# Hybrid decoder step: 128x128 transpositions taken from TensorE, done as 32x32 turns on VectorE and copies through DRAM

## The chip, the cores and the metric

The kernel runs on one core of a Trainium2 chip. The metric is the device time of one execution in microseconds. The median of three runs of the kernel before is 2550.52 us (2545.99 to 2553.72). Its profiled execution took 2546.89 us and has a span of 2545.2 us, from its first instruction to its last.

## The reference, cut to what matters

One layer of a decoder with 16 heads of three kinds over 1024 prompt tokens with 16 meta tokens before them, and 64 sample tokens (8 sequences of 8). All is fp32.

```
h = rmsnorm(x) * norm_w                       # tokens x 2048
proj = h @ w_in                               # 2048 x 8984: q, k, v, o, gates, z of all heads
A, 6 heads: mLSTM scan in chunks (q, k, v, i, f), times sigmoid(o)
B, 6 heads: causal conv of 4, silu, l2norm; gated delta rule (triangular solve per chunk)
C, 4 heads: HGRN2 scan (q, forget f, v)
hcat = concat(A, B, C); hcat *= rsqrt(mean(hcat**2 per head) + eps)
y = hcat * out_norm_w * silu(z)
out = rmsnorm(x + y @ w_out) * final_norm_w   # the states at the end are outputs too
```

## The kernel before, in words

The tokens go in two halves: half 0 has 512 prompt tokens, the 64 sample tokens and the 16 meta tokens (592 columns), half 1 the other 512. The projection keeps channels on partitions and tokens along the columns. A column tile of 128 weights takes four pieces of `w_in` (each 512 x 128, one DMA of 256 KB, `w_raw`, L229). A piece is split into a rounded part `whi` (ScalarE) and a rest `wlo` (VectorE) in `feed_split` (L252). `run_group` (L293) multiplies each 128 x 128 block three times (`whi` with both parts of the input, `wlo` with the first): 24 matmuls of 288 or 304 columns a piece in half 0, 12 of 512 columns in half 1. The splits run up to three pieces ahead of the matmuls and the loads up to seven (`feed_ahead`, L273), in four buffers each. After both halves' projections comes the output product with `w_out` (`oacc`, L1694 on).

Everything else is woven between these matmuls. Each head's scan, its finish and the preparation of half 1's input are Python generators; `Weave` (L145) has four queues of them and lets the first of each take a step, one `yield` long, whenever its due time has come on a planner's clock (`Clock`, L85). The clock adds estimated costs of the instructions written so far; a step is due `LATENCY` = 0.4 us after the last result of the step before, and a step can add to that (`ck.last += 2.0`). `start_head` (L1528) drains the scan of the head before the last and all finishes: there the steps follow each other with no projection matmuls between. All matmuls and transpositions stand in TensorE's one list, all loads and stores in SP's one list, and each engine works through its list in order. All line numbers in the profile's rows are those of a recording helper (L136) for compute, and of the kernel's own line for DMAs.

Where a scan wants tokens on partitions, the tile with channels on partitions is turned by `T.transpose` (a TensorE instruction with the identity, 128 x 128 each) into PSUM, and copied or combined from there. The places that the change touches, per head and half of 512 tokens four transpositions each, and in half 0 one more for the 80 sample and meta tokens:

- `finish` (L799): the normed head outputs `hr` are turned back to channels on partitions (`py`, L818), and VectorE makes `y` from `py`, the weight and the gate `zs` (L820).
- `mlstm_scan` (L924): the values (`pv`, L960; ScalarE copies them to `v1`, L963) and the output gate (`pot`, L971; ScalarE adds 1, L973).
- `hgrn_scan` (L1361): the values (`pvh`, L1462).
- `prep_B` (L598): 16 blocks of half 1's normed input (`pt`, L358), which are split in two parts and stored to DRAM (`hb_dram`), from where `load_hB` (L1596) fetches them before half 1.

Of the kernel before, what the change touches and what calls it, by code (L numbers as in the profile page):

```python
# [189 lines left out]
def hybrid_step(ctx, tc, i, o):  # L190
# [25 lines left out]
    def bank(name):  # L216
        return ps.tile([P, 512], F32, tag="ps", name=name)
# [377 lines left out]
    hb_dram = [dp.tile([NG, P, 4, WB], F32R, name=f"hb{part}") for part in ("hi", "lo")]  # L595


    def prep_B():  # L598
        def load(c, g):
            x = sp.tile([P, 512], F32, tag="px", name="px", bufs=3)  # L600
            DMA(x, i["x_prompt"][0, HALF + P * c:HALF + P * (c + 1), 512 * g:512 * (g + 1)])
            return x

        stats = []
        items = [(c, g) for c in range(NC) for g in range(NG)]
        nxt = load(*items[0])
        for n, (c, g) in enumerate(items):
# [12 lines left out]
        for n, (c, g) in enumerate(items):  # L620
            x = nxt
            if c == 0:
                nw = load_nw(sp.tile([P, 512], F32, tag="pxs", name="pnw", bufs=1), g)
            if n + 1 < len(items):
                nxt = load(*items[n + 1])
            ck.last = ck.t["T"] + 6.0
            yield
            norm_apply(x, P, nw, stats[c])
            ck.last += 2.5
            yield  # L630
            src = transposed(x, P)
            lo = sp.tile([P, 512], F32R, tag="px", name="hblo", bufs=3).rearrange("p (k t) -> p k t", t=P)
            hi = x.bitcast(F32R).rearrange("p (k t) -> p k t", t=P)
            S.copy(hi, src)
            V.tensor_tensor(lo, src, hi, op=ALU.subtract)
# [149 lines left out]
    def evac(half, acc, tag, name, scale=None, func=AF.Copy):  # L785
# [5 lines left out]
                S.activation(t[:, off:off + cnt], a, func, scale=scale)  # L791
        return t

    def square_sums(g, src, ssq):
        for c in range(g.nt):
            scr = sq("scr", "scrq", bufs=1)
            S.activation(scr[:g.n], src[:, c], AF.Square, accum_out=ssq[0:g.n, g.at + c:g.at + c + 1])

    def finish(half, head, outs, ssq, scale, zs):  # L799
        r = sp.tile([P, 16], F32, tag="hr", name="hr")  # L800
        for g in half.groups:
            V.tensor_scalar(r[0:g.n, g.idx], ssq[0:g.n, g.idx], scale / P, EPS, op0=ALU.mult, op1=ALU.add)
            G.tensor_tensor(r[0:g.n, 8 + g.at:8 + g.at + g.nt], r[0:g.n, g.idx], halfneg[0:g.n, 0:g.nt], op=ALU.pow)
        yield
        hrs = []
        for g, hx in zip(half.groups, outs):
# [3 lines left out]
            hrs.append(hr)  # L810
        ck.last += 2.0
        yield
        W = half.width
        y = row("j", "y")
        for g, hr in zip(half.groups, hrs):
            py = bank("py")
            for c in range(g.nt):
                T.transpose(py[:, g.n * c:g.n * (c + 1)], hr[0:g.n, c], ident[0:g.n, 0:g.n])  # L818
            cs = slice(g.c0, g.c0 + g.width)
            V.scalar_tensor_tensor(y[:, cs], py[:, 0:g.width], onw[:, head:head + 1], zs[:, cs], op0=ALU.mult, op1=ALU.mult)  # L820
        yield
        yhi, ylo = zs.bitcast(F32R), y.bitcast(F32R)
        S.copy(yhi[:, 0:W], y[:, 0:W])
        yield
        G.tensor_tensor(ylo[:, 0:W], y[:, 0:W], yhi[:, 0:W], op=ALU.subtract)
        yield
        d = y_dram[half.index][head].bitcast(F32)
        for part, t in enumerate((yhi, ylo)):
            t = t.bitcast(F32)
            at_ = 2 * NSAMP if half.first else 0  # L830
            DMA(d[:, at_ + HALF * part:at_ + HALF * (part + 1)], t[:, 0:HALF])
            if half.first:
                DMA(d[:, NSAMP * part:NSAMP * (part + 1)], t[:, HALF:WS])
# [90 lines left out]
    def mlstm_scan(half, h, kT, qT, vT, tho, zs, nm, em, st):  # L924
# [25 lines left out]
        for g in half.groups:  # L950
            n = g.n
            pk = bank("pk")
            for c in range(g.nt):
                T.transpose(g.psum(pk)[:, c], g.col(kT, c), ident)
            kw = kwall[:, g.idx]
            V.tensor_tensor(kw[0:n], g.psum(pk), gate_col(half, g, K_W, h), op=ALU.mult)
            kws.append(kw)
            pv = bank("pv")
            for c in range(g.nt):
                T.transpose(g.psum(pv)[:, c], g.col(vT, c), ident)  # L960
            v1 = gt("2", g, P + 1)
            G.memset(v1[0:n, :, P:P + 1], 1.0)
            S.copy(v1[0:n, :, 0:P], g.psum(pv))  # L963
            v1s.append(v1)
        ck.last += 2.5
        yield
        for g in half.groups:
            n = g.n
            po = bank("pot")
            for c in range(g.nt):  # L970
                T.transpose(g.psum(po)[:, c], g.col(tho, c), ident)  # L971
            og = gt("3", g)
# [388 lines left out]
    def hgrn_scan(half, h, kT, lf, qT, vT, zs, st):  # L1361
# [181 lines left out]
    def done_tile(half, name, what, acc):  # L1543
# [8 lines left out]
        if what == "z":  # L1552
            t["z"] = no_meta(half, silu_evac(half, acc, "e", "zs"))
            if half.first:
                src = {"A": "state_mlstm_C", "B": "state_gdn_S", "C": "state_hgrn_S"}[kind]
                c["st"] = src
        elif kind == "A":
            if what == "o":
                t["o"] = no_meta(half, evac(half, acc, "d", "tho", scale=0.5, func=AF.Tanh))
            else:  # L1560
                t[what] = evac(half, acc, {"k": "a", "q": "b", "v": "c"}[what], what + "T", scale=KSCALE if what == "k" else None)
                if what == "q":
                    no_meta(half, t[what])
        elif kind == "B":
            weave.drain_queue("post")
            weave.drain(conv_stream)
            ei = {"q": h, "k": HB + h, "v": 2 * HB + h}[what]
            U = conv_evac(half, acc, ei)
            t[what] = row({"k": "c", "q": "d", "v": "f"}[what], "C" + what)
            c["posts"].append(weave.add("post", conv_post(half, U, ei, t[what]), lag="V"))  # L1570
        else:
            if what == "f":
                cf = evac(half, acc, "f", "cf")[:, 0:half.width]
                t["k"], t["f"] = row("a", "hk"), row("g", "lf")
                c["posts"].append(weave.add("post", hgrn_keys(half, h, cf, t["k"], t["f"]), lag="SV"))
            elif what == "q":
                t["q"] = no_meta(half, silu_evac(half, acc, "b", "hq"))
            else:
                t["v"] = evac(half, acc, "c", "hvT")
# [194 lines left out]
```

## Time and profile before

| what | number |
|---|---|
| median of three runs | 2550.52 us (2545.99 to 2553.72) |
| profiled execution, its span | 2546.89 us, 2545.2 us |
| granted TensorE clock, mean | 0.996 of full speed |
| half 0 (0 to 1215 us), TensorE busy | 1171.53 us of 1215 |
| half 1's projections (1215 to 2125 us), TensorE busy | 903.10 us of 910 |
| output product (2125 to 2546 us), TensorE busy | 407.77 us of 421 |
| VectorE, ScalarE busy in half 1's projections | 485.54 us, 368.39 us |

The busy time of an engine is the time covered by at least one of its instructions. Matmuls overlap each other, so a group's busy time and its time per instruction are not what the engine would save without it; that is read from the starts of the instructions around it. "Idle before" is the engine's gap ahead of an instruction, put down to what ended it.

### The profile page before, as it was taken

Reading aid. Unit: us, or ns where it says so; the run is one execution under the profiler, and the core shown is the slowest. Engines: PE = TensorE matmul, PEld = TensorE weight load, DVE = VectorE, ACT = ScalarE, POOL = GpSimd, SP = SyncE. Lnnn points to the kernel's source line nnn. Section 1 sums busy time; section 2 is a strip of 40 time slices with the busy share of each in tenths; the row PEclk is TensorE's granted clock in tenths of the full one; section 3 lists DMA queues with packets and bytes.
Section 4 is the critical chain, followed back from the end, with each engine's and each line's share of the span. In section 5 each row is a group of like instructions: output and inputs, shape, how many; then the busy total and the mean of one; then the engine's idle time right before and its main releaser. Section 6 shows DMA issues by size and latency. Waiting matters only on the chain.

```text
span 2545.2 us, 43177 instructions
## 1 busy us (share of the span) xinstructions
PE 2482.4 (98%) x16022; PEld 2226.0 (87%) x16022; DVE 1376.3 (54%) x2881; ACT 1024.0 (40%) x2512; POOL 552.8 (22%) x722
## 2 busy tenths in 40 slices
PE   6899999999999999999999999999999999999998
PEld 5899999999999999999788888888888888888886
DVE  7665655665745655546754556454554545422435
ACT  5733434343434334334643434333443435322324
POOL 5331212320313312203320103110320102211201
PEclk9999999999999999999999999999999999999999
DMA  5634433555634343436443334433343438436735
GB/s 128 170 91 113 121 85 90 153 154 151 161 79 117 92 119 88 110 88 185 125 118 101 103 99 109 109 98 96 102 106 95 110 97 271 140 84 189 261 97 182
DMA packets 458319, 317.19 MB, mean 125 GB/s; under 512 B 56740, under 2 KB 402428, under 8 KB 457084
## 3 DMA queue, kind: packets, MB, share of 16 engines
q1 hardware_dynamic: 458108, 314.43, 45.7%
q8 instruction: 126, 2.06, 0.3%
q14 instruction: 85, 0.70, 0.1%
HBM read 268.93 MB, written 45.42 MB: 124 GB/s over the span
## 4 chain that ended last, share of the span: by engine, by line
PE 80%; issue 5%; DMA 4%; DVE 4%; POOL 3%; ACT 2%; SPq 0%; POOLq 0%; DVEq 0%; ACTq 0%
PE acc L136 59%; PE oacc L136 8%; PE pa L136 1%; DVE wlo L136 1%; PE po L136 1%; PE pyy L136 1%; PE pz L136 1%; POOL res L136 1%; PE pu L136 1%; PE nd L136 1%; POOL X L136 1%; DMA wraw<-in_w_in_dram 1%; PE poh L136 1%; DMA wraw<-in_w_out_dram 1%; DMA x<-in_x_prompt_dram 1%
## 5 line engine op out<-in xcount | busy, mean ns | idle before, releaser
L136 DVE TENSOR_TENSOR wlo<-wraw,whi 128x512 fp32r<-128x512 f32 x720 | 534.2, 746 | 639.4 <-ACT whi L136 628.3
L136 PE MATMUL acc<-hA,whi 128*128 128x288 f32 (+1 forms) x4544 | 822.9, 303 | 16.1 <-ACT whi L136 10.1
L136 ACT CAST whi<-wraw 128x512 fp32r<-128x512 f32 x720 | 442.2, 618 | 899.0 <-PE acc L136 584.1
L136 PE MATMUL acc<-hB,whi 128*128 128x512 f32 x2272 | 723.3, 400 | 1.5 <-ACT whi L136 1.5
L136 PEld LDWEIGHTS acc<-hA,whi 128*128 128x128 f32 x4544 | 675.4, 190 | 23.2 <-ACT whi L136 12.3
L136 PE MATMUL acc<-hA,wlo 128*128 128x288 f32 x2240 | 487.9, 298 | 0.2 <-DVE wlo L136 0.2
L136 PEld LDWEIGHTS acc<-hB,whi 128*128 128x128 f32 x2272 | 408.8, 188 | 79.7 <-ACT whi L136 3.4
L136 PE MATMUL acc<-hB,wlo 128*128 128x512 f32 x1120 | 439.7, 393 | 2.0 <-DVE wlo L136 2.0
L136 PEld LDWEIGHTS acc<-hA,wlo 128*128 128x128 f32 x2240 | 366.0, 189 | 1.5 <-DVE wlo L136 1.4
L136 PE MATMUL oacc<-whi,y 128*128 128x512 f32 x1088 | 343.8, 390 | 1.2 <-ACT whi L136 1.1
L136 PEld LDWEIGHTS acc<-hB,wlo 128*128 128x128 f32 x1120 | 210.2, 188 | 51.5 <-DVE wlo L136 5.6
L136 PEld LDWEIGHTS oacc<-whi,y 128*128 128x128 f32 x1088 | 204.3, 188 | 44.3 <-ACT whi L136 2.4
L136 PE MATMUL oacc<-wlo,y 128*128 128x512 f32 x576 | 224.6, 390 | 0.8 <-DVE wlo L136 0.7
L136 PEld LDWEIGHTS oacc<-wlo,y 128*128 128x128 f32 x576 | 108.2, 188 | 24.4 <-DVE wlo L136 2.3
L136 POOL TENSOR_TENSOR res<-res,fnw 128x512 f32<-128x512 f32 (+1 forms) x34 | 53.1, 1589 | 259.0 <-ACT oscr L136 259.0
L136 POOL TENSOR_TENSOR qd<-qT,emb 128x512 f32<-128x512 f32 x12 | 16.8, 1401 | 363.7 <-PE po L136 363.7
L136 POOL TENSOR_TENSOR y<-y,zs 128x592 fp32r<-128x592 f32 (+1 forms) x32 | 47.1, 1471 | 143.6 <-ACT zs L136 143.6
L136 DVE TENSOR_TENSOR Yt<-Yc,Bb 128x60 f32<-128x60 f32 (+8 forms) x180 | 36.9, 205 | 51.2 <-DMA Bb<-db 46.5
L136 POOL TENSOR_TENSOR hr<-hr,halfneg 128x4 f32<-128x4 f32 (+1 forms) x48 | 47.2, 984 | 56.0 <-DVE hr L136 55.0
L136 POOL TENSOR_TENSOR X<-Ex,hk 128x256 f32<-128x256 f32 (+1 forms) x40 | 38.5, 963 | 93.2 <-PE pa L136 75.5
L136 POOL TENSOR_TENSOR nrm<-nrm,halfneg 128x10 f32<-128x10 f32 x12 | 23.5, 1956 | 129.3 <-DVE nrm L136 129.3
L136 DVE TENSOR_TENSOR Sx<-Sx,lf 128x256 f32<-128x256 f32 (+2 forms) x60 | 34.0, 569 | 26.9 <-ACT Ex L136 24.9
(410 smaller groups left out, 2839.6 us busy)
## 6 DMA issues: line engine op xcount, KB each, us to landing
wraw<-in_w_in_dram SPq DMA_DIRECT2D x564, 256.0 KB
wraw<-in_w_out_dram SPq DMA_DIRECT2D x144, 256.0 KB
y<-y SPq DMA_DIRECT2D x16, 576.0 KB
px<-in_x_prompt_dram SPq DMA_DIRECT2D x32, 256.0 KB
out_dram<-sst SPq DMA_DIRECT2D x16, 512.0 KB
y<-zs SPq DMA_DIRECT2D x32, 256.0 KB
y<-y SPq DMA_DIRECT2D x32, 256.0 KB
res<-in_x_prompt_dram SPq DMA_DIRECT2D x32, 256.0 KB
```

Of the source, the lines that this page charges most:

```text
L136: return f(out, *a, **k)
```

## The change

The transpositions of the 512 prompt tokens at the four places leave TensorE; those of the 80 sample and meta tokens stay. In their place VectorE turns each 32 x 32 block on its own (`V.transpose`, named STREAM_TRANSPOSE in a program's rows), four DMAs store the tile to a DRAM scratch tensor with pieces of 32 elements (`turn_out`), and one DMA loads it back with the blocks in their places (`turn_in`). For values and output gates the turn is made when the projection's result is read out of PSUM (`turned_evac`), and the gate's tanh moves behind the load. In `finish` the chain gets one more step: turn and store, then load, then `y` at least 5 us later on the planner's clock. In `prep_B` the turned block is split and stored by 4 + 4 DMAs in place of 1 + 1, and the scratch's shape puts the blocks in place.

```
 # shapes: SQ = 32, NQ = 4
-hb_dram = [dp.tile([NG, P, 4, WB], ...)]
+hb_dram = [dp.tile([NG, 4 * NQ, SQ, WB], ...)]
 # prep_B
-src = transposed(x, P)
-lo = sp.tile([P, 512], F32R, tag="px", name="hblo", bufs=3)...
+src = sp.tile([P, 512], F32, tag="px", name="xT", bufs=3)
+V.transpose(src, x)
+hi, lo = x.bitcast(F32R), src.bitcast(F32R)
 S.copy(hi, src)
 V.tensor_tensor(lo, src, hi, op=ALU.subtract)
 for t, d in ((hi, hb_dram[0]), (lo, hb_dram[1])):
-    DMA(d[g, :, :, P * c:P * (c + 1)].bitcast(F32), t.bitcast(F32))
+    for q in range(NQ):
+        at_ = P * c + SQ * q
+        DMA(d[g, :, :, at_:at_ + SQ]....rearrange("x j i -> j x i"),
+            t[SQ * q:SQ * (q + 1)]....rearrange("p (x i) -> p x i", i=SQ))
 # new
+def turn_out(t, name):
+    d = dp.tile([NC * NQ, SQ, NQ, SQ], F32, name=name)
+    for q in range(NQ):
+        DMA(d[:, :, q].rearrange("x j i -> j x i"), t[SQ * q:SQ * (q + 1), 0:HALF].rearrange("p (x i) -> p x i", i=SQ))
+    return d
+def turn_in(dst, d):
+    DMA(dst, d.rearrange("(c b) j a i -> (b j) c (a i)", b=NQ))
+def turned_evac(half, acc, tag, name, small):
+    t = row(tag, name)
+    for a, off, cnt in spans(half, acc):
+        n = min(cnt, HALF - off)
+        V.transpose(t[:, off:off + n], a[:, 0:n])
+        if n < cnt:
+            small(t[:, HALF:off + cnt], a[:, n:cnt])
+    return t, turn_out(t, scratch_name(name))
 # finish
+y = row("j", "y")
+V.transpose(y[:, 0:HALF], hrs[-1].rearrange("p c e -> p (c e)"))
+d = turn_out(y, scratch_name("yd"))
 ck.last += 2.0
 yield
+turn_in(hrs[-1], d)
+ck.last = ck.t["T"] + 5.0
+yield
 for g, hr in zip(half.groups, hrs):
-    py = bank("py")
-    for c in range(g.nt):
-        T.transpose(py[:, g.n * c:g.n * (c + 1)], hr[0:g.n, c], ident[0:g.n, 0:g.n])
+    (small group: as before)  else: src = hr
-    V.scalar_tensor_tensor(y[:, cs], py[:, 0:g.width], onw[:, head:head + 1], zs[:, cs], ...)
+    V.scalar_tensor_tensor(y[:, cs], src, onw[:, head:head + 1], zs[:, cs], ...)
 # mlstm_scan, main group (small group as before)
-    T.transpose(g.psum(pv)[:, c], g.col(vT, c), ident)
-S.copy(v1[0:n, :, 0:P], g.psum(pv))
+    turn_in(v1[:, :, 0:P], vT[1])
+    og = gt("3", g)
+    turn_in(og, tho[1])
 ...
-    T.transpose(g.psum(po)[:, c], g.col(tho, c), ident)
-S.activation(og[0:n], g.psum(po), AF.Copy, bias=1.0)
+S.activation(og, og, AF.Tanh, scale=0.5)
+S.activation(og, og, AF.Copy, bias=1.0)
 # hgrn_scan, main group
-    T.transpose(g.psum(pt)[:, c], g.col(vT, c), ident)
-S.copy(v[0:g.n], g.psum(pt))
+    turn_in(v, vT[1])
 # done_tile
-"o", "v" of A and "v" of C: evac(half, acc, ...)
+"o", "v" of A and "v" of C: turned_evac(half, acc, ...)
 # load_hB
-DMA(hB[g][part].bitcast(F32), hb_dram[part][g].bitcast(F32))
+DMA(hB[g][part].bitcast(F32), hb_dram[part][g].bitcast(F32).rearrange("(k b) j t -> (b j) k t", b=NQ))
```

In TensorE's list, at the second A head of half 0, where the scan is drained (`acc` the projection, `py` head outputs, `pot` output gates, `pum` the state update, `nd` the scan's outputs, `pu` the update of the sample states), before and now:

```order
L136 MATMUL acc<-hA_88,wlo 128x304
L136 MATMUL py<-ident,t_5225 128x80
L136 MATMUL py<-ident,s_5227 128x128 x4
L136 MATMUL pot<-ident,tho 80x128
L136 MATMUL pot<-ident,tho 128x128 x4
L136 MATMUL pum<-meta_725,kwall 128x137
L136 MATMUL pum<-s_5254,kwall 128x129 x4
L136 MATMUL nd<-sst,spread_723 32x129 x8
...
L136 MATMUL nd<-state_A_741,qd 128x129
...
L136 MATMUL nd<-s_5254,s_5203 128x129
L136 MATMUL acc<-hA_82,whi 128x288 x2
```

```order
L138 MATMUL acc<-hA_88,wlo 128x304
L138 MATMUL pot<-ident,tho 80x128
L138 MATMUL pum<-meta_725,kwall 128x137
L138 MATMUL pum<-s_5279,kwall 128x129 x4
L138 MATMUL nd<-sst,spread_723 32x129 x8
...
L138 MATMUL py<-ident,t_5248 128x80
L138 MATMUL nd<-state_A_741,qd 128x129
...
L138 MATMUL nd<-s_5279,s_5226 128x129
L138 MATMUL pu<-vx,k_5403 128x512
L138 MATMUL acc<-hA_82,whi 128x288 x2
```

The two groups of four transpositions (`x4`) are gone, those of the sample and meta tokens stay; `py` has moved behind the first `nd`, and a `pu`, which stood behind projection matmuls, now follows the last `nd` at once. In the built list the six A heads of half 0 are all drained from `pot` to the last `nd` now (five of them wholly before), with a `pu` behind it at five, and at two of them (one before) `pst` and `pk` stand in the drained row as well.

In VectorE's list, where the third A head of half 1 starts its scan and the head before it finishes (`wlo` the split of a weight piece, `hr` the norm factor, `zs` the gate, `pst` scores, `kwall` keys, `pum` state update), before and now:

```order
L136 TENSOR_TENSOR s_19424<-s_18933,hr 128x512
L136 TENSOR_TENSOR wlo<-wraw,whi 128x512
L136 SCALAR_TENSOR_TENSOR zs<-zs,acc 128x512
L136 TENSOR_TENSOR wlo<-wraw,whi 128x512
L136 TENSOR_TENSOR s_19441<-s_19441,pst 128x512
L136 TENSOR_TENSOR wlo<-wraw,whi 128x512
L136 SCALAR_TENSOR_TENSOR y<-py,onw,zs 128x512
L136 TENSOR_TENSOR kwall<-pk,cols 128x512
```

```order
L138 STREAM_TRANSPOSE y<-s_19542 128x512
L138 TENSOR_TENSOR wlo<-wraw,whi 128x512
L138 TENSOR_TENSOR s_19566<-s_19566,pst 128x512
L138 TENSOR_TENSOR wlo<-wraw,whi 128x512
L138 TENSOR_TENSOR kwall<-pk,cols 128x512
L138 TENSOR_TENSOR wlo<-wraw,whi 128x512
L138 SCALAR_TENSOR_TENSOR s_19634<-state_A_742,emb,pum 128x129
L138 SCALAR_TENSOR_TENSOR s_19634<-s_19634,emb,pum 128x129 x3
L138 TENSOR_TENSOR wlo<-wraw,whi 128x512
L138 SCALAR_TENSOR_TENSOR y<-s_19542,onw,zs 128x512
```

The turn of `y` now stands four splits ahead of the product that makes `y`, and that product reads the tile that the load has refilled.

In SP's list at that same place (`eGb`, `emb`: gate rows; `y_761` the scratch for all heads' `y`; `yd`, `tho`, `vT` the new scratch tensors), before and now:

```order
L771 DMA eGb<-rows_759 128x512
L237 DMA wraw<-in_w_in_dram 128x4x128 x3
L831 DMA y_761<-zs 128x512
L831 DMA y_761<-y 128x512
L237 DMA wraw<-in_w_in_dram 128x4x128
L771 DMA emb<-rows_759 128x512
```

```order
L809 DMA s_19599<-tho_19378 128x4x128
L239 DMA wraw<-in_w_in_dram 128x4x128
L809 DMA s_19596<-vT_19230 128x4x128
L1385 DMA out_dram<-state_B_748 128x128
L778 DMA eGb<-rows_759 128x512
L239 DMA wraw<-in_w_in_dram 128x4x128
L805 DMA yd_19546<-y 32x16x32 x4
L239 DMA wraw<-in_w_in_dram 128x4x128 x3
L809 DMA s_19542<-yd_19546 128x4x128
```

The four stores of `yd` stand three weight loads ahead of the load that fetches it back; the loads of the gate and the values stand ahead of both.

## Rows read from the trace of the kernel before

**Rows 1.** The page: busy time by engine, and the chain's shares.
```profile
PE 2482.4 (98%) x16022; PEld 2226.0 (87%) x16022; DVE 1376.3 (54%) x2881; ACT 1024.0 (40%) x2512; POOL 552.8 (22%) x722
...
PE 80%; issue 5%; DMA 4%; DVE 4%; POOL 3%; ACT 2%; SPq 0%; POOLq 0%; DVEq 0%; ACTq 0%
```

**Rows 2.** TensorE's groups by form, transpositions (busy us, mean ns | idle).
```profile
L136 PE MATMUL py<-ident,s 128*128 128x128 f32 x128 | 19.2, 272 | 0.9 <-DVE s L136 0.9
...
L136 PE MATMUL pt<-ident,px 128*128 128x128 f32 x64 | 9.6, 273 | 0.0
...
L136 PE MATMUL pv<-ident,vT 128*128 128x128 f32 x48 | 7.2, 273 | 0.0
...
L136 PE MATMUL pot<-ident,tho 128*128 128x128 f32 x48 | 7.2, 272 | 0.0
...
L136 PE MATMUL pvh<-ident,hvT 128*128 128x128 f32 x32 | 5.0, 280 | 0.0
```

**Rows 3.** Timeline, half 1, TensorE (start us, us): transpositions among projection matmuls.
```profile
1315.95 0.62 PE L136 MATMUL acc<-hB,whi 128*128 128x512 f32 x2
...
1316.64 0.62 PE L136 MATMUL acc<-hB,whi 128*128 128x512 f32 x2
...
1317.33 0.60 PE L136 MATMUL py<-ident,s 128*128 128x128 f32 x4
1317.69 0.71 PE L136 MATMUL acc<-hB,whi 128*128 128x512 f32 x2
...
1318.47 0.62 PE L136 MATMUL acc<-hB,whi 128*128 128x512 f32 x2
```

**Rows 4.** Timeline, half 0: transpositions in a row, a wait behind them.
```profile
426.28 0.60 PE L136 MATMUL py<-ident,s 128*128 128x128 f32 x4
...
426.72 0.71 PE L136 MATMUL pot<-ident,tho 128*80 128x128 f32 x5
...
432.59 0.46 PE L136 MATMUL nd<-s,qd 128*128 128x129 f32 x2 [1.41 <-DVE s L136]
```

**Rows 5.** Waits of TensorE: total us, times, longest.
```profile
PE acc L136 <- ACT whi L136: 11.6, 12, 2.1
...
PE nd L136 <- DVE s L136: 4.1, 3, 1.4
```

**Rows 6.** Waits of the other engines: the same columns.
```profile
ACT whi L136 <- PE acc L136: 584.1, 325, 4.2
...
DVE Yt L136 <- DMA Bb<-db: 46.5, 12, 5.1
```

**Rows 7.** The chain that ended last, merged: start us, us, matmuls in a row.
```profile
717.90 17.70 PE acc L136 x132
```

**Rows 8.** Groups of VectorE by form (busy us, mean ns), for the turn.
```profile
L136 DVE COPY nw<-pnw 128x512 f32<-128x512 f32 x4 | 2.5, 683 | 2.6 <-PE pnw L136 2.6
...
L136 DVE MEMSET wraw<- 128x512 f32 x12 | 5.8, 485 | 1.5 <-PEq L1762 1.0
```

**Rows 9.** Timeline in half 1: small stores to DRAM, loads back, their first reader.
```profile
1334.60 5.06 SPq L1157 DMA_DIRECT2D db<-Ball  x8
...
1341.06 1.91 SPq L1163 DMA_DIRECT2D Bb<-db  x3
...
1345.32 0.22 DVE L136 TENSOR_TENSOR Yt<-Yc,Bb 128x60 f32<-128x60 f32 x1 [4.10 <-DMA Bb<-db]
```

**Rows 10.** Stretches: length; PE, PEld, DVE, ACT, POOL busy; clock, DMA share, GB/s.
```profile
0.00:1215.00 1215.00, 1171.53 (x9240) 1140.85 (x9241) 718.71 (x1619) 513.72 (x1371) 316.09 (x487) 0.99 0.47 122
1336.50:1341.00 4.50, 4.50 (x24) 3.74 (x24) 2.33 (x4) 1.90 (x5) 0.00 (x0) 1.00 0.07 7
1341.00:1349.00 8.00, 8.00 (x37) 6.62 (x36) 3.52 (x16) 2.35 (x4) 0.64 (x1) 1.00 0.72 209
```

**Rows 11.** The page: the DMA queue of SP, packets, MB, share of 16 engines.
```profile
q1 hardware_dynamic: 458108, 314.43, 45.7%
```

**Rows 12.** Waits of SP's queue.
```profile
SPq L237 <- DVE wlo L136: 799.2, 320, 7.9
```

More of the change, by code (lines that the diff above doesn't have):

```diff
@@ L31 @@
 SUB = 16
+SQ = 32
+NQ = P // SQ
 UW = NB * (NS + 3) + 3 + NMETA + HALF
@@ L594, in hybrid_step @@
     y_dram = [dp.tile([NH, P, w], F32R, name=f"y{w}") for w in (2 * NSAMP + 2 * HALF, 2 * HALF)]
-    hb_dram = [dp.tile([NG, P, 4, WB], F32R, name=f"hb{part}") for part in ("hi", "lo")]
+    hb_dram = [dp.tile([NG, 4 * NQ, SQ, WB], F32R, name=f"hb{part}") for part in ("hi", "lo")]
     def prep_B():
@@ L810, in finish @@
             hrs.append(hr)
+        y = row("j", "y")
+        main = half.main
+        V.transpose(y[:, 0:HALF], hrs[-1].rearrange("p c e -> p (c e)"))
+        d = turn_out(y, scratch_name("yd"))
         ck.last += 2.0
@@ L813, in finish @@
         W = half.width
-        y = row("j", "y")
+        turn_in(hrs[-1], d)
+        ck.last = ck.t["T"] + 5.0
+        yield
         for g, hr in zip(half.groups, hrs):
-            py = bank("py")
-            for c in range(g.nt):
-                T.transpose(py[:, g.n * c:g.n * (c + 1)], hr[0:g.n, c], ident[0:g.n, 0:g.n])
             cs = slice(g.c0, g.c0 + g.width)
-            V.scalar_tensor_tensor(y[:, cs], py[:, 0:g.width], onw[:, head:head + 1], zs[:, cs], op0=ALU.mult, op1=ALU.mult)
+            if g.small:
+                py = bank("py")
+                T.transpose(py[:, 0:g.n], hr[0:g.n, 0], ident[0:g.n, 0:g.n])
+                src = py[:, 0:g.n]
+            else:
+                src = hr.rearrange("p c t -> p (c t)")
+            V.scalar_tensor_tensor(y[:, cs], src, onw[:, head:head + 1], zs[:, cs], op0=ALU.mult, op1=ALU.mult)
         yield
@@ L957, in mlstm_scan @@
             kws.append(kw)
-            pv = bank("pv")
-            for c in range(g.nt):
-                T.transpose(g.psum(pv)[:, c], g.col(vT, c), ident)
             v1 = gt("2", g, P + 1)
             G.memset(v1[0:n, :, P:P + 1], 1.0)
-            S.copy(v1[0:n, :, 0:P], g.psum(pv))
+            if g.small:
+                pv = bank("pv")
+                T.transpose(g.psum(pv)[:, 0], g.col(vT[0], 0), ident)
+                S.copy(v1[0:n, :, 0:P], g.psum(pv))
+            else:
+                turn_in(v1[:, :, 0:P], vT[1])
+                og = gt("3", g)
+                turn_in(og, tho[1])
             v1s.append(v1)
@@ L968, in mlstm_scan @@
             n = g.n
-            po = bank("pot")
-            for c in range(g.nt):
-                T.transpose(g.psum(po)[:, c], g.col(tho, c), ident)
-            og = gt("3", g)
-            S.activation(og[0:n], g.psum(po), AF.Copy, bias=1.0)
+            if g.small:
+                po = bank("pot")
+                T.transpose(g.psum(po)[:, 0], g.col(tho[0], 0), ident)
+                ogs.append(gt("3", g))
+                S.activation(ogs[0][0:n], g.psum(po), AF.Copy, bias=1.0)
+                continue
+            S.activation(og, og, AF.Tanh, scale=0.5)
+            S.activation(og, og, AF.Copy, bias=1.0)
             ogs.append(og)
@@ L1459, in hgrn_scan @@
         for g in gs:
-            pt = bank("pvh")
-            for c in range(g.nt):
-                T.transpose(g.psum(pt)[:, c], g.col(vT, c), ident)
             v = gt("2", g)
-            S.copy(v[0:g.n], g.psum(pt))
+            if g.small:
+                pt = bank("pvh")
+                T.transpose(g.psum(pt)[:, 0], g.col(vT[0], 0), ident)
+                S.copy(v[0:g.n], g.psum(pt))
+            else:
+                turn_in(v, vT[1])
             vs.append(v)
@@ L1558, in done_tile @@
             if what == "o":
-                t["o"] = no_meta(half, evac(half, acc, "d", "tho", scale=0.5, func=AF.Tanh))
+                row_, d = turned_evac(half, acc, "d", "tho", lambda dst, src: S.activation(dst, src, AF.Tanh, scale=0.5))
+                t["o"] = no_meta(half, row_), d
+            elif what == "v":
+                t["v"] = turned_evac(half, acc, "c", "vT", S.copy)
             else:
-                t[what] = evac(half, acc, {"k": "a", "q": "b", "v": "c"}[what], what + "T", scale=KSCALE if what == "k" else None)
+                t[what] = evac(half, acc, {"k": "a", "q": "b"}[what], what + "T", scale=KSCALE if what == "k" else None)
                 if what == "q":
@@ L1578, in done_tile @@
             else:
-                t["v"] = evac(half, acc, "c", "hvT")
+                t["v"] = turned_evac(half, acc, "c", "hvT", S.copy)
         if what == "z":
```

10 lines of the change are left out of this document (8 added, 2 removed).

## Prediction

> **What bounds the kernel now.** I read the page's busy times first: TensorE is busy 98% of the span and its share of the chain that ended last is 80%; VectorE has 54%, ScalarE 40% [rows 1]. A busy TensorE need not be TensorE at its peak, so the waits come next. TensorE's own list of waits is short: the projection waited for ScalarE's splits 11.6 us in all, the mLSTM outputs for VectorE 4.1 us [rows 5]. On the other side ScalarE waited 584.1 us, 325 times, for projection matmuls to give a split buffer back [rows 6]: the splits run ahead of TensorE, not behind it. A stretch of 132 projection matmuls took 17.70 us [rows 7], 0.134 us each, so a piece of half 0 (24 matmuls) lasts 3.2 us; in half 1 three matmuls take 0.69 us [rows 3], so a piece of 12 lasts 2.8 us. With splits up to three pieces ahead, VectorE or ScalarE can be late by some 8 us before TensorE notices. So TensorE's time is the kernel's time, and what leaves its list is a gain unless something new makes it wait.
>
> **TensorE's part.** Four transpositions leave at each of 80 places: 32 in `finish`, 16 in `prep_B`, 12 for values and 12 for gates of the mLSTM heads, 8 for values of the HGRN heads: 128 + 64 + 48 + 48 + 32 = 320 instructions, the counts of [rows 2]. The busy times there add up to 48.2 us (19.2 + 9.6 + 7.2 + 7.2 + 5.0), but each instruction's 272 ns overlap the next one's. The starts tell what they cost. Between projection matmuls: the normal step of three is 0.69 us (1315.95 to 1316.64), with four transpositions in it 1.05 us (1316.64 to 1317.69), and the step after it 0.78 us (1317.69 to 1318.47) [rows 3]. That is 0.36 + 0.09 = 0.45 us a place. In a row with other small matmuls four take 0.44 us (426.28 to 426.72) [rows 4]. So 80 x 0.45 = 36 us leave, bounds 35 (80 x 0.44) and 48 (all the busy time); I take 36.
>
> The Trainium skill (TensorE: Matmul & The Clock Gate, Part 4: PE-mode transpose) gives about 275 ns for one such transposition inside a kernel. The rows have that duration, 272 ns, but its product with 320, 88 us, is not what leaves: by the starts one costs 0.11 us.
>
> **VectorE's part.** 96 turns are added: 64 of 128 x 512 (32 for `y`, 16 in `prep_B`, 16 in half 1) and, for the two column spans of half 0, 16 of 128 x 288 and 16 of 128 x 224. No row has a turn. The nearest from below is a fill of 128 x 512, 0.485 us, from above a copy out of PSUM of that size, 0.683 us [rows 8]; even if a turn took twice the copy, 96 x 1.37 = 131 us. I take the copy, at most 96 x 0.683 = 66 us. The reading of the turned output is the same product as before, from SBUF instead of PSUM. In half 0 VectorE is busy 718.7 of 1215 us [rows 10], 59%, and would be at 62%. ScalarE loses the copies of values and a gate's read-out and gains a tanh and a copy of it. All of it lies beside TensorE: 0 on the path. The cover is the 8 us of lead; a delay beyond it would be paid in full.
>
> **The way through DRAM.** It has the form of one that is there already: `db` is written by eight small stores (5.06 us to issue, 0.63 each), the loads `Bb` are issued 1.4 us after the last store's issue (1339.66 to 1341.06), 0.64 each, and VectorE starts on them 2.35 us after their last issue (1342.97 to 1345.32) [rows 9]. For `y`: four stores 2.5, landing 1.4, one load 0.64, landing 2.35, so 6.9 us, and the time of 2048 pieces of 128 bytes on 16 engines. From below: the stretch with the small stores has a DMA share of 0.07 over 4.5 us of 16 engines [rows 10], 5.0 us for their 512 pieces of 64 bytes and whatever else, 10 ns a piece, so 1.3 us. From above: the mean packet, 45.7% of 16 x 2545.2 us over 458108 packets [rows 11], 40.6 ns, so 5.2 us. The trip takes 8.2 to 12.1 us; I take 8.2, since small pieces are what is moved. VectorE's list has four splits between the turn and the product that needs the load, each at a piece's pace of 2.8 us in half 1: 8.3 us for three steps, 11 us for four. So the product waits between nothing and 3.8 us. Such a wait costs TensorE nothing: VectorE waited 4.10 us for `Bb` (12 times, at most 5.1 us [rows 6, 9]), and TensorE was busy 8.00 of 8 us around it [rows 10]. I take 0; without the cover it would be 32 x 3.8 = 122 us.
>
> The values and gates are stored when the projection tile is read out, and SP's list has their loads ahead of the stores of `y`; the state update (`pum`, or `puh` for HGRN) needs them, by the built list, 30 projection matmuls behind the scores in half 1, 6.9 us. I take 0; if TensorE met each load at its issue, 20 heads and halves x (0.64 + 2.35) = 60 us.
>
> **SP and the DMA engines.** New DMAs: 4 + 1 for each of 64 trips, 320, and 6 more at each of 16 blocks, 96: 416 x 0.63 = 262 us of SP. SP waited 799.2 us in front of weight loads for the splits that free their buffers [rows 12], so it has the time; a weight load queued behind a `turn_in` that waits for its stores has four buffers of lead, 11 us. Bytes: 64 x 2048 pieces out, 64 x 512 in (40.6 ns each), 65,536 pieces in `prep_B` for 16,384 before. By 10 ns a small piece it is 82 + 83 + 41 - 42 = 164 us, by 40.6 ns it is 333 + 83 + 166 - 42 = 540 us: a share of 52 to 67% for 46 now. Cost 0.
>
> **Half 0's drained rows.** There the finish is two steps and 8 us longer on the planner's clock, so every drain now empties the scan up to the last `nd`, with nothing behind which a wait could hide. A wait of 1.41 us stands there now [rows 4], three in all [rows 5]. Six such, and 2 us at each of the two heads whose keys (`pk`) fall into the drained row too: 6 x 1.4 + 4 - 4.1 = 8 us. Bounds: -4.1 (the waits go) and six of the longest wait for a load, 6 x 5.1 = 31. I take 6, nearer to the three waits that a row shows than to a load's.
>
> **Sum.** 2546.9 - 36 + 6 = 2517 us against the profiled execution, which is 3.6 us under the median of 2550.5. Forecast: 2520 us.
>
> **Rivals.** (1) Given back: TensorE, which met only PSUM and ScalarE here, now meets loads. For it: `pum` and `puh` wait for a DMA directly, and half 0 loses 1215 - 1171.5 = 43.5 us of TensorE already [rows 10]. Against: the distances above. With 1.5 us at 20 heads and halves, 30 us: 2550 us. (2) Slower: the trip for `y` holds VectorE, and the splits behind it. It decides from a trip of 8.3 us (the list's distance) + 8.3 us (TensorE's lead) = 16.6 us. If the stores queue behind three weight loads (512 packets each, 1.3 us, so 3.9), each issue takes twice 0.63 (2.5 more) and pieces cost 40.6 ns (3.9 more), a trip is 18.5 us, and 32 x 1.9 = 61 us are paid: 2581 us. Against it: [rows 9] shows no such queue. (3) The pieces are the price: each trip's data take 19 times 1.3 us, 25 us; a trip of 32 us would be over the lead by 15 us, 32 times, 480 us: about 3000 us. The pieces of [rows 10] at 10 ns or less speak against it. The Trainium skill (VectorE: DVE Perf Modes, The three transpose paths) warns of that: a plain DMA whose strides do the transposing is 19 times slower than the transposing path. By that rule rival 3 comes about; the rule speaks of a large stride in the innermost dimension, here runs of 32 elements stay whole, and no run here shows the other path. (4) More: all 48 us leave and the drains cost nothing: 2502 us.
>
> **How the numbers follow.** What differs by less than 0.3%, 7.6 us, can't be told from no change here. The forecast's own case, 2508 to 2531 us, has 0.58; a part given back, 2531 to 2543, 0.18; rival 1, 0.12; rival 2, 0.07; rival 3, 0.02; rival 4, 0.03. Faster 0.58 + 0.18 + 0.03 = 0.79, same 0.12, slower 0.09. The range of 2506 to 2548 us holds the first two and about half of rival 1, and leaves out rivals 2 and 3.
>
> **What would show it.** TensorE with 320 matmuls fewer, a busy time some 35 us lower and still 98% of its span; turns of 128 x 512 at 0.5 to 0.8 us; VectorE's waits for `s` from `yd` under 4 us each and no new TensorE row behind them; a DMA share of 50 to 67%. Wrong would be: TensorE rows that wait for `vT` or `tho` scratch loads (rival 1), VectorE waits for `yd` over 16 us or ScalarE no longer waiting for `acc` (rival 2), a DMA share near 1 in the stores' stretches (rival 3).

## The result, and the profile after

| | before | changed |
|---|---|---|
| median of four runs (us) | 2549.1 | 2525.3 |
| lowest to highest (us) | 2546.0 to 2553.7 | 2524.8 to 2527.5 |
| ratio, 95% interval | 1 | 0.9907 (0.9890 to 0.9924) |
| span of the profiled execution (us) | 2545.2 | 2523.4 |

The change saves 23.8 us; the forecast was 30.5 (2520 us for 2550.5). The page of the changed kernel answers to [rows 1, 11] (busy time by engine; the chain's shares; the DMA queue with packets, MB and share of the 16 engines):

```profile
PE 2456.8 (97%) x15702; PEld 2199.6 (87%) x15702; DVE 1427.0 (57%) x2977; ACT 1012.3 (40%) x2476; POOL 555.0 (22%) x722
...
q1 hardware_dynamic: 680828, 348.01, 53.9%
...
PE 74%; DMA 6%; issue 6%; DVE 5%; ACT 4%; POOL 3%; SPq 1%; POOLq 0%; DVEq 0%; ACTq 0%
```

TensorE has 320 matmuls fewer, but its busy time fell by only 25.6 us where the removed work was put at 36. So the first question is not who waits, but where 10 us of busy time came from. The groups of VectorE by form (busy us, mean ns | idle before, releaser) show the new operation, which no row of before had:

```profile
L138 DVE SCALAR_TENSOR_TENSOR y<-s,onw,zs 128x512 f32<-128x512 f32 x32 | 25.1, 784 | 5.6 <-DMA s<-yd 3.9 <-DMA hblo<-xT 1.7
...
L138 DVE STREAM_TRANSPOSE y<-s 128x512 f32<-128x512 f32 x32 | 22.6, 706 | 0.4
...
L138 DVE STREAM_TRANSPOSE xT<-px 128x512 f32<-128x512 f32 x16 | 11.3, 705 | 1.2 <-DMA hblo<-xT 1.2
...
L138 DVE STREAM_TRANSPOSE tho<-acc 128x288 f32<-128x288 f32 x6 | 2.9, 483 | 11.7 <-PE acc L138 11.7
L138 DVE STREAM_TRANSPOSE tho<-acc 128x224 f32<-128x224 f32 x6 | 2.2, 374 | 0.0
```

A turn of 128 x 512 takes 0.705 us from SBUF. The product that reads the turned output runs 32 times (16 heads, two halves) and waited 3.9 us in all for its loads. The waits (us in total, times, longest) answer to [rows 5, 6, 12]:

```profile
PE acc L138 <- ACT whi L138: 10.2, 8, 3.0
PE acc L138 <- DVE wlo L138: 6.9, 8, 1.4
PE nd L138 <- DVE s L138: 4.8, 4, 1.8
...
PE oacc L138 <- DVE wlo L138: 2.1, 4, 1.4
PE pum L138 <- ACT v L138: 2.0, 2, 1.0
...
PE nd L138 <- DVE nsT L138: 1.6, 4, 1.1
...
PE acc L138 <- DMA hB<-hblo: 0.9, 1, 0.9
...
DVE y L138 <- DMA s<-yd: 3.9, 8, 1.6
...
ACT whi L138 <- PE acc L138: 570.2, 313, 4.3
...
SPq L239 <- DVE wlo L138: 606.2, 282, 6.7
```

No TensorE row waits for the loads of values or gates. For the loads of half 1's input (`hB`), which now passes through the pieces, it waited 0.9 us for one part and 0.3 us for the other, and before it had no such row. What else is new is small and spread: TensorE waits for VectorE's half of the split (`wlo`) 6.9 + 2.1 us, where before it was 2.2 + 0.7. The decisive view is the stretches (length; PE, PEld, DVE, ACT, POOL busy; granted clock, DMA share, GB/s). The first row runs from the first `pan` matmul to TensorE's last; the other eight are four pairs, a stretch with the clock at 1.00 and a wait in it, and the one that follows:

```profile
131.40:2513.00 2381.60, 2351.67 (x15051) 2101.99 (x15049) 1327.18 (x2763) 929.06 (x2292) 499.19 (x585) 1.00 0.54 138
194.80:201.60 6.80, 5.45 (x38) 4.73 (x37) 2.70 (x7) 2.04 (x7) 3.43 (x3) 1.00 0.54 133
201.60:208.50 6.90, 6.20 (x27) 6.20 (x28) 3.53 (x7) 2.22 (x7) 2.23 (x4) 0.51 0.46 133
290.00:293.80 3.80, 1.98 (x14) 1.76 (x15) 3.79 (x8) 0.00 (x0) 2.68 (x3) 1.00 0.04 4
293.80:297.20 3.40, 3.40 (x15) 3.30 (x15) 3.40 (x15) 2.55 (x9) 1.09 (x2) 0.50 0.76 193
1195.00:1201.80 6.80, 5.17 (x58) 3.91 (x56) 2.75 (x7) 3.10 (x10) 1.28 (x1) 1.00 1.01 237
1201.80:1208.60 6.80, 4.21 (x9) 2.91 (x10) 5.05 (x10) 3.14 (x8) 1.04 (x1) 0.50 0.30 77
2126.80:2130.20 3.40, 1.60 (x7) 0.78 (x5) 3.19 (x5) 2.68 (x6) 3.40 (x5) 1.00 0.72 165
2130.20:2133.60 3.40, 3.40 (x8) 2.69 (x9) 3.40 (x5) 1.30 (x3) 2.50 (x3) 0.50 0.50 118
```

Four times TensorE waits 1.8 to 3.0 us, in one to three pieces that may reach into the second stretch of the pair, and in that second stretch its granted clock is 0.50, the lower of its two levels (1.2 instead of 2.4 GHz). There it is busy 6.20 + 3.40 + 4.21 + 3.40 = 17.2 us and does the work of 8.6: 8.6 us are lost that count as busy. Before the change no such stretch lies behind the first `pan` matmul (135.5 us). That is not for want of waits. In the trace of before, TensorE waited 2.57 us up to 587.47 us, and the clock stayed at 1.00 (the same columns):

```profile
584.90:587.50 2.60, 0.03 (x1) 0.06 (x2) 2.50 (x8) 0.00 (x0) 0.41 (x1) 1.00 0.21 68
587.50:592.00 4.50, 4.50 (x36) 4.50 (x37) 2.78 (x6) 1.12 (x3) 0.00 (x0) 1.00 0.57 137
```

So a wait of this length can lower the clock and need not. Two pieces of the changed kernel's timeline follow (start us, us, engine, operation, idle before and its releaser): the largest of the waits, and an output's trip through DRAM.

```profile
1198.53 0.59 ACT L138 COPY both<-acc 128x512 f32<-128x512 f32 x1 [8.27 <-PE acc L138]
...
1199.97 0.49 PE L138 MATMUL puh<-meta,t 80*128 80x128 f32 x2 [0.29 <-ACT meta L138]
...
1202.83 2.18 ACT L138 CAST whi<-wraw 128x512 fp32r<-128x512 f32 x4
...
1203.50 1.22 PE L138 MATMUL acc<-hB,whi 128*128 128x512 f32 x2 [3.04 <-ACT whi L138]
...
1302.16 0.71 DVE L138 STREAM_TRANSPOSE y<-s 128x512 f32<-128x512 f32 x1
...
1302.90 0.34 SPq L805 DMA_DIRECT2D yd<-y  x1
...
1303.90 1.59 SPq L805 DMA_DIRECT2D yd<-y  x3
...
1308.41 0.38 SPq L809 DMA_DIRECT2D s<-yd  x1
...
1314.84 0.74 DVE L138 SCALAR_TENSOR_TENSOR y<-s,onw,zs 128x512 f32<-128x512 f32 x1
```

At 1302 the trip of an output begins, and the product reads it 12 us later without a wait. At 1198 ScalarE, which works in order, waits 8.27 us for a projection's last matmul; then come the small copies of a drained scan, and only at 1202.83 the splits that TensorE needs.

### The profile page after: what moved, and what is told of

The parts are those of the page before. It is cut to its first block, busy times and chain, and to the rows that moved or that the text cites. A ratio compares the mean times of both kernels' runs of the same rounds, so it can differ in the third digit from the quotient of the medians.

```text
span 2523.4 us, 43205 instructions
## 1 busy us (share of the span) xinstructions
PE 2456.8 (97%) x15702; PEld 2199.6 (87%) x15702; DVE 1427.0 (57%) x2977; ACT 1012.3 (40%) x2476; POOL 555.0 (22%) x722
## 2 busy tenths in 40 slices
DMA packets 681041, 350.77 MB, mean 139 GB/s; under 512 B 260004, under 2 KB 622076, under 8 KB 680828
## 3 DMA queue, kind: packets, MB, share of 16 engines
q1 hardware_dynamic: 680828, 348.01, 53.9%
## 4 chain that ended last, share of the span: by engine, by line
PE 74%; DMA 6%; issue 6%; DVE 5%; ACT 4%; POOL 3%; SPq 1%; POOLq 0%; DVEq 0%; ACTq 0%
PE acc L138 55%; PE oacc L138 8%; PE pa L138 1%; DVE wlo L138 1%; DMA wraw<-in_w_in_dram 1%; PE po L138 1%; POOL X L138 1%; PE pyy L138 1%; PE pz L138 1%; POOL res L138 1%; ACT whi L138 1%; PE pu L138 1%; ACT L138 1%; PE poh L138 1%; PE nd L138 1%
## 5 line engine op out<-in xcount | busy, mean ns | idle before, releaser
L138 DVE TENSOR_TENSOR wlo<-wraw,whi 128x512 fp32r<-128x512 f32 x720 | 528.4, 738 | 584.9 <-ACT whi L138 566.0
L138 DVE TENSOR_TENSOR Sx<-Sx,lf 128x256 f32<-128x256 f32 (+2 forms) x60 | 36.5, 613 | 20.2 <-ACT Ex L138 19.1
```

What stands on the lines that cost most here:

```text
L138: return f(out, *a, **k)
```

## The experiments

From each trace three numbers are worked out, over the stretch from the first `pan` matmul to TensorE's last: its busy time, the half of its busy time at 0.50 ("clock"), and the idle time between its matmuls ("waits"). Work is busy time less clock. The same 652 matmuls stand ahead of the first `pan` matmul in every kernel here but the last two of the table. Work still compares only to about 8 us: an instruction's modelled end can lie behind the next one's start, so short waits count as busy. before_lead4, with the same matmuls as before, has 7.9 us less work, and the steps between its projection matmuls exceed 133 and 227 ns by 7 us less in all. Each row is one execution's; its time can lie some us from the median (after_again's 4.9 below it, lat_02's 5.3 above).

| kernel | median us | ratio to before (95%) | work | clock | waits |
|---|---|---|---|---|---|
| before | 2549.1 | 1 | 2377.1 | 0 | 22.1 |
| changed | 2525.3 | 0.9907 (0.9890 to 0.9924) | 2343.1 | 8.6 | 29.9 |
| after_again | 2525.4 | 0.9904 (0.9889 to 0.9918) | 2342.4 | 7.3 | 26.4 |
| y_only | 2539.0 | 0.9969 (0.9958 to 0.9979) | 2360.0 | 5.5 | 27.7 |
| values_gates_only | 2539.5 | 0.9971 (0.9961 to 0.9980) | 2364.1 | 7.7 | 33.3 |
| input_only | 2538.9 | 0.9966 (0.9956 to 0.9977) | 2368.7 | 0 | 20.2 |
| fill4 | 2525.4 | 0.9911 (0.9896 to 0.9926) | 2352.2 | 3.4 | 27.3 |
| notrips | 2550.3 | 1.0008 (0.9998 to 1.0017) | 2342.7 | 15.1 | 42.0 |
| keep | 2594.3 | 1.0177 (1.0162 to 1.0192) | 2379.7 | 15.0 | 59.0 |
| lead4 | 2522.4 | 0.9905 (0.9888 to 0.9922) | 2338.4 | 8.8 | 30.4 |
| before_lead4 | 2542.1 | 0.9976 (0.9965 to 0.9986) | 2369.2 | 3.4 | 15.3 |
| double_trip | 2539.6 | 0.9966 (0.9955 to 0.9977) | 2344.8 | 11.6 | 41.3 |
| lat_02 | 2535.0 | 0.9955 (0.9941 to 0.9969) | 2350.8 | 13.6 | 34.0 |
| lat_08 | 2567.5 | 1.0074 (1.0060 to 1.0089) | 2346.5 | 18.8 | 56.7 |

**One part alone.** Three kernels take the hunks of the diff one at a time: `finish`; the values and gates; `prep_B` with `hb_dram` and `load_hB`.

> Only the outputs of the heads (32 of the 80 places) leave TensorE; values, gates and the second half's input stay on it as before. Theory (each place gives back 0.45 us of TensorE; what was lost again in the whole change were new stretches at half of the granted clock behind waits of 2 to 3 us): 32 x 0.455 = 14.6 us faster than before, about 2534.5 us, plus 1.4 to 3.2 us for each stretch at half rate after the first 130 us that the profile of before does not have; TensorE's busy time outside such stretches falls by about 14 us. Rival (the DRAM trips and the turns slow all of TensorE's work evenly, so that a place is worth about 0.3 us): 32 x 0.3 = 9.6 us, about 2539.5 us, without new stretches at half rate, the 512-column pitch of the projections of the second half visibly above 227 ns.

> Only the values and the output gates (32 of the 80 places) leave TensorE; outputs and the second half's input stay on it. Theory: 32 x 0.455 = 14.6 us faster, about 2534.5 us, plus 1.4 to 3.2 us for each new stretch at half rate. Rival (slowed evenly): about 2539.5 us without such stretches.

> Only the second half's input (16 of the 80 places) leaves TensorE. Theory: 16 x 0.455 = 7.3 us faster, about 2542 us, plus 1.4 to 3.2 us for each new stretch at half rate; if the four stretches of the whole change come from single places of the plan, they need not appear here. Rival (slowed evenly; this part has 128 of the 128-byte-piece stores): 16 x 0.3 = 4.8 us, about 2544 us, no such stretch.

They save 9.1, 8.5 and 9.1 us (each median against that of its own runs of before, 2548.0), 26.7 in sum for 23.8 together. The times of the first two fit the theory (with its stretches) and the rival nearly alike, and the third saved more than either forecast. By the work 17.1, 12.9 and 8.3 us went, where the theory had 14.6, 14.6 and 7.3 and the rival 9.6, 9.6 and 4.8. At 8 us of uncertainty no one part decides; the sum, 38.3, is nearer to the theory's 36.5 than to the rival's 24. The first two give part of it back through two and four new stretches at half rate and 6 to 11 us more waits; the third has neither and keeps all. The profile of values_gates_only is of an execution of 2547.9 us, 8.4 above its median, so its waits may be too high. The rival falls by its own signs: such stretches are there, and the median distance of two projection matmuls is 227 ns in half 1 and 133 ns in half 0 in the traces of before, of the change, and of y_only.

**The change again, and TensorE kept busy in the four waits.**

```
 pk = bank("pkk")
+if half.first and h == 0: fill(pk[:, 0:P], 8 if g.small else 6)
 nd = bank("nd")
+if half.first and h == 0 and not g.small: fill(nd[:, 0:P], 15 if c0 else 9)
 T.matmul(pu[:, 0:P], kk[0:NT0, 0], meta_rows(v[:, 0])[0:NT0, 0:P], ...)
+if h == HC - 1: fill(pu[:, 2 * P:3 * P], 25)
+if half.first and cg == 0 and k == 3 and n == 0: fill(bank("fill")[:, 0:P], 12)
 T.matmul(accs[n], yh, wlo, ...)
```

> The changed kernel itself, as the reference for the three kernels beside it. Theory (the four stretches at half of the granted clock belong to waits that the order of the work sets): they come again at about 202, 294, 1202 and 2130 us, 8.6 us of TensorE's work lost in them, and the time is 2525 us within 3. Rival (they are chance): other places, another number of them, and a time that moves by 1.7 us for each 3.4 us of half rate.

> The changed kernel with 75 more transpositions of the identity matrix on TensorE, read by nobody, in the four waits ahead of those stretches (8 and 6 at 200 us, 9 and 15 at 289 and 291, 25 at 1200, 12 at 2128: each a little shorter than the wait at 0.11 us apiece). Theory (TensorE's idle time pulls the granted clock down, and the work behind pays): the four stretches are gone, 8.6 us less than the changed kernel, about 2516.5 us (2513 to 2520). Rival 1 (the clock falls for another reason, such as the DMA traffic): the stretches stay, 2525 us or, where the dummies are late, up to 8 us more. Rival 2 (the waits only look short of work, and the engines behind them are late in any case): stretches gone but other waits longer, 2522 to 2525 us.

The order of all other instructions is the same. The change again had stretches at half rate at 140, 205, 294 and 1201 us: three of the four places, one new. At 2130 us the clock stayed at 1.00, though the same wait (1.8 us) stood there. With the dummies the four old ones are gone; the stretches behind the filled waits:

```profile
203.30:209.50 6.20, 6.20 (x52) 6.04 (x56) 4.56 (x9) 2.90 (x9) 1.47 (x4) 1.00 0.56 155
...
293.90:297.40 3.50, 3.50 (x28) 3.45 (x27) 3.50 (x11) 1.58 (x5) 1.80 (x2) 1.00 0.70 186
...
1202.50:1208.60 6.10, 4.20 (x23) 3.18 (x24) 4.48 (x11) 2.69 (x6) 0.00 (x0) 1.00 0.41 107
...
2132.00:2135.50 3.50, 3.39 (x16) 2.66 (x15) 3.50 (x6) 1.34 (x4) 2.63 (x3) 1.00 0.40 117
```

So at the three places where both executions of the change had the stretch, TensorE's idle time is what pulled its clock down; 23 matmuls run at 1202.5 where 9 ran without the dummies. Yet the time stayed at 2525.4 us: rival 2. The dummies count as work now, 75 x 0.11 = 8.2 us (9.1 by the table), in place of about as much waiting. But the waits in all are only 2.6 us lower than in the first execution of the change and 0.9 higher than in the second, so other waits came in their place, and with two new stretches the clock still costs 3.4 us. The list of the same kernel:

```profile
PE acc L138 <- DVE wlo L138: 9.3, 13, 1.6
PE acc L138 <- ACT whi L138: 8.3, 9, 2.3
...
PE nd L138 <- DVE nsT L138: 2.9, 3, 2.5
```

The `nd` wait of 2.5 us is in the next mLSTM head, with a stretch at half rate behind it (435.6 us), where the change waited 1.0 us and had none. That a faster TensorE meets engines that were late anyway would explain this; it is not shown wait by wait.

**The trips away, or the transpositions kept.** In notrips the turned blocks are read where they lie; in keep TensorE still turns everything as well.

```
-turn_in(hrs[-1], d)
-src = hr.rearrange("p c t -> p (c t)")
+src = y[:, cs]                              # notrips
...
+T.transpose(py[:, g.n * c:g.n * (c + 1)], y[:, P * c:P * (c + 1)], ident)   # keep
```

> The changed kernel without any of the new trips through DRAM: VectorE turns the 32x32 blocks, and the blocks are used where they lie (so outputs, values, gates and the second half's input are not in their places; the ones' columns of the values are filled in by GpSimd with the rest); the second half's input is stored and loaded whole, as before the change. Theory (the pieces cost TensorE nothing but waits): TensorE's work without clock losses stays within 3 us of the changed kernel's; the time falls by no more than the waits that the trips end (about 4 us on VectorE, 1 to 2 on TensorE) and what clock they cost, to 2515 to 2525 us. Rival (the DMA traffic of 128-byte pieces slows weight loads and matmuls): the work falls by 8 us or more at unchanged waits, 2512 us or less.

> The changed kernel in which TensorE still does all 320 transpositions at the old places, into banks that nobody reads: the turns, the trips and the pieces stay. Theory (a place is worth 0.45 us of TensorE's work, and turns and trips cost about 8 us of waits and 9 of clock): work 34 to 38 us above the changed kernel's, 2555 to 2563 us. Rival 1 (the turns and trips cost nothing at all): 2549 us, that of before. Rival 2 (a place is worth 0.3 us, since the weight loads behind hide the rest): 24 us above, about 2549 us, by the work and not by the waits.

Work separates what the times blur. Without the trips it is 2342.7 us, with them 2342.4 and 2343.1: the pieces slow no matmul. With the transpositions kept it is 37 us higher, 0.46 to 0.47 us a place. Both times missed every expectation, by waits and clock. Beside the kernel before, keep does the same work (2.6 us more) and is 45 us slower, with 36.9 us more waits and 15.0 us of clock. So turns and trips are hidden in the changed kernel's order, and not in this one; what the kept transpositions themselves wait for is not separated from it. notrips was no clean test: with the second half's input stored whole, VectorE's turn in `prep_B` waits for the previous store to free its buffer, 11.3 us between 100 and 470 us, where the change has 1.2; it also fills more memory on GpSimd. Keep also shows the wait that the prediction had priced and dismissed (start us, us):

```profile
685.66 4.87 SPq L806 DMA_DIRECT2D yd<-y  x4
690.63 0.55 SPq L810 DMA_DIRECT2D s<-vT  x1
...
693.85 2.06 PE L138 MATMUL pum<-s,kwall 128*128 128x129 f32 x8 [14.10 <-DMA s<-vT]
```

The load of the values stands on SP's queue behind a run of other DMAs, the last of them four stores of another head's output (4.87 us). TensorE's order met it here and pays 14.1 us for one load.

**Splits further ahead.**

```
-feed_split(p + 3)
-feed_raw(p + 7)
+feed_split(min(p + 4, len(raws)))        # whi, wlo: bufs=5
+feed_raw(p + 8)
```

> The changed kernel with the weight pieces split four ahead instead of three (five buffers of whi and wlo, the raw piece loaded one earlier; 32 bytes a partition come from a small tile that is single now). Theory (late splits are what VectorE's and ScalarE's new work costs: after the first 130 us the matmuls of the changed kernel wait 13.5 us for whi and wlo, 7.9 us before the change, and two of its four stretches at half rate follow such waits): most of the 13.5 us and 2.1 + 1.7 us of clock go, 2508 to 2514 us, TensorE's work unchanged. Rival (ScalarE and VectorE work in order, and what stands ahead of a split there waits for TensorE itself; a longer lead only moves the wait): 2521 to 2526 us.

> The same longer lead in the kernel before, as its control. Theory: at most its 7.9 us of waits for whi and wlo go, no stretch at half rate, 2541 to 2545 us, so that the gap to the changed kernel grows to about 30 us. Rival: 2546 to 2550 us.

The control gained 5.6 us (2547.6 to 2542.1), though it has two stretches at half rate where none was expected. The changed kernel gained 3 us of its own median, within its intervals, so with the longer lead in both the change is worth 19.7 us. The waits of TensorE in lead4:

```profile
PE acc L138 <- ACT whi L138: 6.1, 4, 2.5
PE poh L138 <- DVE s L138: 6.0, 1, 6.0
...
PE pa L138 <- ACT U L138: 5.0, 1, 5.0
...
PE px L138 <- DVE bb L138: 3.7, 1, 3.7
...
PE acc L138 <- DVE wlo L138: 2.5, 4, 0.8
```

The waits for `whi` and `wlo` fall from 17.1 to 8.6 us, and three waits of 3.7 to 6.0 us stand there instead: with splits put ahead, the scans' own steps come later on the same in-order engines. In the longest, VectorE worked through three splits (from 1214.46, 1217.35 and 1218.39 us) before the `s` that TensorE waited for. The rival holds.

**The trip doubled.**

```
 turn_in(hrs[-1], d)
+DMA(again, hrs[-1].rearrange("p c t -> p (c t)"))
+DMA(hrs[-1].rearrange("p c t -> p (c t)"), again)
```

> The changed kernel with each head's output sent through DRAM once more after it has been put in place (32 more stores and loads of 256 KB, one behind the other), the plan's distance of 5 us unchanged: the trip is about doubled, 8.2 to 12.1 us becoming 16 to 24 us. Theory of the prediction (VectorE's waits are covered by the splits' lead only up to a trip of 16.6 us): VectorE waits 3 to 10 us a head for the output, TensorE waits for wlo in many heads, 30 to 100 us slower than the changed kernel. Rival (the planner's and the streams' slack is larger than the lead, or the wait falls where VectorE has nothing else to do): under 10 us slower.

It costs 14.2 us (2539.6 for 2525.4), between the two. VectorE's wait is much smaller than expected:

```profile
DVE y L138 <- DMA s<-again: 22.8, 13, 4.0
```

13 of the 32 products wait, at most 4.0 us. From the end of the turn to the product it is now 18.3 us in the median (13.1 to 28.2), for 11.2 (9.5 to 15.7) in the changed kernel. A trip of that length is still mostly hidden; what it costs is 11 to 15 us more waits of TensorE, spread, and 3 to 4 us of clock.

**The same instructions in another order.** `LATENCY`, the planner's pause behind a step, is 0.2 or 0.8 instead of 0.4.

> The changed kernel with the planner's pause after each step 0.2 us instead of 0.4: the same instructions in another order (1174 rows of TensorE's listing differ). Theory (TensorE's work is fixed by what the kernel computes, 2342 us after the first 130; waits and half rate together, 34 to 38 us there, depend on where the order puts each step): work within 3 us, waits and clock between 25 and 55 us, so 2513 to 2543 us, with the stretches at half rate at other places. Rival (the order does not matter much, the waits come from VectorE's and ScalarE's load): within 4 us of 2525 us.

> The same with a pause of 0.8 us (1870 rows differ). Theory: work within 3 us of the changed kernel's, waits and clock between 25 and 55 us, 2513 to 2543 us; fewer waits of TensorE for nd, pum and pkk, since steps come later, and longer drains at the end of the first half. Rival: within 4 us of 2525 us.

2535.0 and 2567.5 us: +10 and +42 us for one number, from slower than the forecast's own case to slower than before. By the work they are 8 and 3 us off. lat_02 has 598 matmuls ahead of the marker, 54 fewer, which is 7.2 us at 0.134 each; lat_08 has 664, 12 more, or 1.6 us. So for the same matmuls they are 0.5 and 5 us off, the second over the theory's 3. Waits and clock go from 38.5 us to 47.6 and 75.5. The second is outside the theory's range too, which ended at 55: a bound that was too tight. In it TensorE meets loads too:

```profile
PE acc L138 <- ACT whi L138: 12.2, 10, 3.5
...
PE pkT L138 <- DVE t L138: 6.6, 2, 5.9
PE px L138 <- DVE s L138: 6.6, 3, 3.8
...
PE puh L138 <- DMA s<-hvT: 4.4, 1, 4.4
```

None of these versions beats the changed kernel by more than the intervals.

## Why the prediction was right, and the term that it lacked

- **TensorE's part (-36 us): right.** Work fell by 34.0 us (34.7 in the second execution), 0.43 us a place; kept transpositions cost 37 us. Reading the cost off the starts instead of the durations was what made it so. The prediction read one place; the 19 places of the trace before with projection matmuls on both sides give 0.45 us in the median too. The Trainium skill (TensorE: Matmul & The Clock Gate, Part 4: PE-mode transpose) gives 275 ns a transposition and names bf16; the durations here, in fp32, are 272 ns and agree with it. By that figure 320 of them would be an estimated 88 us, and 34 went.
- **VectorE's part (0): right in size, nearly in cost.** Turns took 0.705 us, for 0.683 taken; in all 58.9 us for at most 66. But TensorE's waits for `wlo` rose from 2.9 to 9.0 us. Four of the seven in the projection behind the first `pan` stand where VectorE works on HGRN's gate (`lf`, `Sx`), as all five of before do, so the lead seems to be exceeded where it was short already; which part of it the turns cause was not tested.
- **The trip (0): right in this order.** VectorE waited 3.9 us for `yd` in all, at most 1.6. Rival 2 put the point of decision at 16.6 us, with every head paying beyond it; the doubled trip, 18.3 us in the median where rival 2 had 18.5, shows that it was built too rigidly: it costs 14 us, not 61. Rival 3 set a factor of 19 on the pieces and had a trip of 32 us. The Trainium skill (VectorE: DVE Perf Modes, The three transpose paths) states that factor for a plain DMA that transposes by its strides, against the DMA's own transposing path, where the innermost stride is large. With runs of 128 bytes no such price is seen: the output stored from 1302.90 us on is read at 1314.84, 12 us later.
- **SP and the DMA engines (0): right here, by the order.** Share 53.9% in the forecast's 52 to 67%; TensorE met no load of values or gates, and 1.2 us of `hB`, which the step did not price. The distance of the loads was read from the list, and with another order one load cost 14.1 us, in lat_08 another 4.4.
- **The drained rows (+6): right in size by luck, wrong in place.** Waits grew by 7.8 us (4.3 the second time). For the `nd` rows that the step spoke of it was 1.9 us (`s` 4.1 to 4.8, `nsT` 0.4 to 1.6); the larger part is `wlo`, which the sum had at nothing.
- **What the sum lacked: +8.6 us of clock** (7.3 the second time). The step on the drained rows counted each wait by its own length; at four waits TensorE also ran at half rate, and that shows as busy time, not as a wait. The stretch ahead of the first `pan` matmul was 4.1 us shorter (3.3). So -34.0 + 7.8 + 8.6 - 4.1 = -21.7 us, the difference of the two spans. The 8.6 us are those of two executions, though. The kernel before had a mean granted clock of 0.996 in the profiled one, but of 0.9936 on average in 59 others (0.991 to 0.997); the changed kernel had 0.9921 on average in its eight (0.990 to 0.993). The averages lie about 0.0015 apart, some 4 us of the span, the two profiled executions 0.0044, some 11 us. So by this estimate the change costs less clock than 8.6 us in a usual execution; where the others lost theirs is not on record.

That the clock cost nearly as much as the four waits (8.6 us for 9.7) is shown for the one trace, not as a rule: waits of about 2 us stood elsewhere with the clock at 1.00 (2.57 us before the change, 1.98 us at 136.45 in the changed kernel). That it could be had back is not shown: with the dummies it went, and new waits took its place. Why notrips is slower by 25 us than the change is shown only as far as its waits go; a kernel without the trips but with the change's own input path was not tried.

## What to carry to other kernels

When TensorE has 97% of the span, split its time into work, half rate and waits before judging a change. Of the three only the work fell by what the edit removed. Four waits of 1.8 to 3.0 us (9.7 in all) cost 8.6 us more by the clock here, others as long cost nothing more. In a kernel whose order is planned by hand, the same instructions in another order moved the time by 10 and 42 us, the second more than this change; so a gain of 1% has to be measured, and the planner's numbers tried again after it. Loads that the order hides are hidden by that order alone: note on which queue they stand, and behind what.

## What the runs showed of the hardware

- VectorE's turn of 32 x 32 blocks in fp32 takes 0.705 us for 128 x 512 from SBUF, 0.717 from PSUM, 0.483 for 288 columns and 0.374 for 224.
- 222,720 more packets in the profiled execution (680,828 for 458,108), most of them pieces of 128 bytes, raised the DMA share from 45.7 to 53.9%, and the distance of projection matmuls stayed at 227 and 133 ns.
- The granted clock went to 0.50 at four waits of TensorE (1.8 to 3.0 us, in one to three pieces) and back to 1.00 after 3.4 to 6.9 us; with dummy transpositions in the same waits it stayed at 1.00. At waits of 2.57 us (before) and 1.98 us (the change, at 136.45) it stayed at 1.00 without them, and the wait of 1.8 us ahead of 2130 us lowered it in one execution of the changed kernel and not in the other.
